# Hybrid decoder block on one core: sparse attention in single key blocks, transposes and products as steps of their own, the first unit beside the last query tile, the compressed product in 128 rows

## The chip, the core and the metric

The kernel runs on one core of a Trainium2 chip. The engines are TensorE (PE, with its weight loads listed as PEld), VectorE (DVE), ScalarE (ACT), GpSimd (POOL) and SyncE (SP), which issues the DMAs. Each engine works through its own queue in the order in which it was written. The metric is the device time of one execution in microseconds, the median over runs.

## The reference

One layer of a decoder block on 1024 tokens with 1024 channels. Two branches read one projection of x: a gated delta rule (o_a, 512 channels) and native sparse attention (o_b, 512 channels). With 16 blocks of 64 keys in the sequence and the 16 best chosen, every block is chosen, so the selected branch is plain causal attention over all keys.

```python
def masked_softmax(s, mask):
    s = jnp.where(mask, s.astype(jnp.float32), -jnp.inf)
    m = jnp.max(s, axis=-1, keepdims=True)
    p = jnp.exp(s - jnp.where(jnp.isfinite(m), m, 0.0))
    d = jnp.sum(p, axis=-1, keepdims=True)
    return p / jnp.where(d > 0, d, 1.0)
...
kc = compress(k_c, pos_k, w1_k, w2_k)          # 63 compressed keys and values
vc = compress(v_c, pos_v, w1_v, w2_v)
p_cmp = masked_softmax(q @ kc, cmp_end <= pos)     # 8 query heads on 2 key heads, 64 channels each
o_cmp = p_cmp @ vc
o_slc = masked_softmax(q @ ks, kpos <= pos) @ vs   # the selected blocks
o_win = masked_softmax(q @ kw, (kpos <= pos) & (kpos > pos - 512)) @ vw
o_b = gt[..., 0:1] * o_cmp + gt[..., 1:2] * o_slc + gt[..., 2:3] * o_win
...
mixed = sigmoid(gate_a) * (o_a @ w_branch_gdn) + sigmoid(gate_b) * (o_b @ w_branch_nsa)
h = layer_norm(DN_ALPHA * x + mixed @ w_out, ln1_g, ln1_b)
u = causal_dwconv(h @ w_up, ffn_conv_w)
u_g, u_v = split(u, 2)
x = layer_norm(DN_ALPHA * h + (silu(u_g) * u_v) @ w_down, ln2_g, ln2_b)
```

## The kernel before

A float32 value is handled as a high and a low part, both in the type that PE takes at full speed; a product is high x high, low x high and high x low. Names that end in h and l, or wh and wl, are such pairs.

The stages follow one another: projections and the delta rule (to about 604 us), the last query tile `q_tile(3)` beside the compression of the values `comp_c("v")` (to 628), the attention (to about 892), the two branch products (to 982), the product with w_out and the norm, the feed-forward (to 1708), and the last norm.

The attention runs over 16 units (t, g): a tile t of 128 queries and a key head g with its four query heads r. The order is `UNITS`: t = 1 to 7, and t = 0 last. A unit has three branches: b = 0, the selected one, over all keys up to its own; b = 1, the window, over at most 640 keys; and the compressed one, over 64 columns.

- `score_steps` makes the scores of one branch. `kS` holds the keys with their high and low halves stacked in 128 rows, `qS` the queries likewise; each head takes two products for its keys (two again where there are more than 512), and a product of the identity with a mask from `am`. DVE takes the maximum (L912), ACT the exponential into P (L914), then DVE the reciprocal of the sum, and `scale` multiplies P by it, on POOL (L876) or ACT (L872) in a rotation, `SCALE`.
- `cmp_scores` does it for the compressed keys (`khc`, `klc`), with two clamps of the statistics (L934, L939), and POOL scales `Pc` (L941).
- `pv_steps` makes an item for each block of 128 keys and one for the compressed ones: four transposes of P on PE into a small PSUM bank (L949), a copy to the high part wh on ACT (L951), a subtraction to the low part wl on DVE (L952), and two products with `vS`, which holds the value's high and low halves side by side. For the compressed item all that has 64 rows and the values are `vC`. The products are held back by `LAG` = 2 items. `weave` lays the items of the unit before among the score steps of a unit. `fin` adds the two halves into `oB`.
- `down_sums` uses POOL (L999) to prepare differences of w_down for the feed-forward, one piece at a time.
- Beside the last unit's items comes the first branch product, `branch(0, 0)`, `Y0` = 4 matmuls ahead of each item. Its inputs are the high and low parts of o_a (`oAh`, `oAl`), split by `half_split` (L1033 to L1036) on ACT, DVE and POOL, and weights that `load_ab` loads, casts on ACT (L1051) and subtracts on POOL (L1052). Then `oB` is split too, and the rest of the branches follow; `use` multiplies by the gates on DVE (L1065).

PSUM has big banks of 1024 columns (`big`) and small ones of 512 (`sm`). Tiles with the tag "wh" or "wl" share a ring of three buffers each; a tile waits until the last use of the one that had its buffer. Inside `manual_schedule` a program orders each engine's queue. The profile names L192, a helper, for every product.

## Time and profile before

| what | value |
|---|---|
| median of 3 runs | 1729.74 us (1729.28 to 1729.77) |
| profiled execution | 1731.17 us |
| its span, first to last instruction | 1729.5 us |
| mean granted clock of TensorE | 0.991 |
| PE busy | 1684.3 us, 97% |
| DVE busy | 1153.4 us, 67% |
| ACT busy | 743.6 us, 43% |
| POOL busy | 783.1 us, 45% |
| DMA moved | 189.90 MB |

The profile is of one execution. The busy time of PE counts the modelled ends of its matmuls: in a run without waits a product of 512 columns shows 0.39 us, and the next one starts 0.23 us after it. So starts, rather than durations, tell what a product costs. The releaser in square brackets is what the profile takes to have ended an engine's idle time. A granted clock of 1.00 is 2.4 GHz, 0.5 is 1.2 GHz.

### The profile page before, as it was taken

What the parts mean: (1) busy time and instruction counts of PE and PEld (TensorE: products, weight loads), DVE (VectorE), ACT (ScalarE), POOL (GpSimd) and SP (SyncE); (2) the same over time, 40 slices, a digit from 0 to 9 for tenths busy, and PEclk for the clock granted to TensorE, in tenths of its full rate; (3) what the DMA queues carried; (4) which work ended last, traced back from release to release, by engine and by line L of the source; (5) the groups of instructions that cost most, each with busy time, mean ns of one, the idle gap of its engine ahead of it and who ended that gap; (6) DMA issues with size and microseconds to landing.
All of it is one profiled execution on the core that took longest, in us unless ns stands there. A gap on an engine that the chain in (4) does not pass through costs nothing.

```text
span 1729.5 us, 23653 instructions
## 1 busy us (share of the span) xinstructions
PE 1684.3 (97%) x8578; PEld 1412.4 (82%) x8578; DVE 1153.4 (67%) x2148; ACT 743.6 (43%) x1280; POOL 783.1 (45%) x650
## 2 busy tenths in 40 slices
PE   8999999999999999999989999999999999999997
PEld 8888888888888877788868787778888888888885
DVE  3556767677644359999863328988777767865756
ACT  3422323323213458788853114544444444543333
POOL 1322222222222537876458226687787777200005
PEclk9999999999999999999999999999999999999998
DMA  5222122121321323333026612333332233597722
GB/s 176 74 63 76 56 61 57 52 75 32 88 80 51 98 88 113 120 118 103 8 85 189 220 49 98 97 122 100 120 116 92 98 103 105 190 362 237 231 94 98
DMA packets 196722, 189.90 MB, mean 110 GB/s; under 512 B 19400, under 2 KB 154749, under 8 KB 196605
## 3 DMA queue, kind: packets, MB, share of 16 engines
q1 hardware_dynamic: 196605, 188.39, 34.3%
q8 instruction: 68, 1.11, 0.3%
q14 instruction: 49, 0.40, 0.1%
HBM read 136.97 MB, written 51.38 MB: 109 GB/s over the span
## 4 chain that ended last, share of the span: by engine, by line
PE 84%; DVE 7%; issue 3%; ACT 3%; POOL 2%; DMA 1%; SPq 0%; ACTq 0%; POOLq 0%; DVEq 0%
PE pq L192 34%; PE big L192 33%; PE sm L192 13%; PE sm L949 3%; DVE st L912 1%; ACT P L914 1%; DVE wl L952 1%; DVE wb L1396 0%; POOL h L1253 0%; POOL hr L1725 0%; POOL h L1254 0%; DMA w<-in_w_out_dram 0%; DVE accs L1407 0%; DMA w<-in_w_in_dram 0%; ACT wh L951 0%
## 5 line engine op out<-in xcount | busy, mean ns | idle before, releaser
L182 POOL TENSOR_TENSOR wl<-w,wh 128x1024 fp32r<-128x1024 f32 (+2 forms) x51 | 123.1, 2420 | 362.0 <-PE big L192 131.0
L192 PE MATMUL big<-xTl,wh 128*128 128x512 f32 x624 | 250.6, 402 | 0.0
L192 PE MATMUL big<-xTh,wh 128*128 128x512 f32 x624 | 250.3, 401 | 0.0
L192 PE MATMUL pq<-wd 128*128 128x512 f32 x924 | 209.6, 389 | 0.0
L192 PEld LDWEIGHTS pq<-wd 128*128 128x128 f32 x924 | 173.5, 188 | 36.0
L192 PE MATMUL pq<-xb,wb 128*128 128x512 f32 x792 | 187.6, 391 | 2.1 <-DVE accs L1407 1.5
L1407 DVE SCALAR_TENSOR_TENSOR accs<-pq,fcw,accs 128x511 f32<-128x511 f32 (+3 forms) x264 | 144.3, 568 | 61.0 <-ACT accs L1495 56.1
L192 PEld LDWEIGHTS pq<-xb,wb 128*128 128x128 f32 x792 | 148.5, 188 | 34.8 <-issue 2.9
L192 PE MATMUL big<-xTh,wl 128*128 128x512 f32 x624 | 164.1, 399 | 0.0
L192 PEld LDWEIGHTS big<-xTl,wh 128*128 128x128 f32 x624 | 117.7, 189 | 21.3 <-issue 0.2
L192 PEld LDWEIGHTS big<-xTh,wh 128*128 128x128 f32 x624 | 117.7, 189 | 21.2
L192 PEld LDWEIGHTS big<-xTh,wl 128*128 128x128 f32 x624 | 114.0, 188 | 22.0
L192 PE MATMUL pq<-mTh,wb 128*128 128x512 f32 x528 | 126.1, 394 | 3.2 <-ACT mTh L1195 3.1
L192 PE MATMUL pq<-mTl,wb 128*128 128x512 f32 x528 | 127.3, 391 | 0.0
L876 POOL TENSOR_TENSOR P<-P,st 128x640 f32<-128x640 f32 (+7 forms) x96 | 99.8, 1068 | 52.6 <-DVE st L885 20.7
L192 PEld LDWEIGHTS pq<-mTh,wb 128*128 128x128 f32 x528 | 100.0, 190 | 25.4 <-ACT mTh L1195 3.3
L192 PEld LDWEIGHTS pq<-mTl,wb 128*128 128x128 f32 x528 | 99.1, 188 | 21.2
L1396 POOL TENSOR_TENSOR wb<-w,wb 128x512 fp32r<-128x512 f32 x79 | 103.5, 1316 | 27.4 <-ACT wb L1195 27.4
L181 ACT ACTIVATE wh<-w 128x1024 fp32r<-128x1024 f32 (+2 forms) x51 | 53.0, 1046 | 128.1 <-PE big L192 85.9
L952 DVE TENSOR_TENSOR wl<-sm,wh 128x512 fp32r<-128x512 f32 (+1 forms) x148 | 99.4, 682 | 10.3 <-ACT wh L951 8.0
L951 ACT ACTIVATE wh<-sm 128x512 fp32r<-128x512 f32 (+1 forms) x148 | 87.1, 595 | 22.7 <-PE sm L949 19.1
L914 ACT ACTIVATE P<-big,st 128x640 f32<-128x640 f32 (+7 forms) x128 | 88.8, 701 | 10.3 <-DVE st L912 9.6
(381 smaller groups left out, 3599.0 us busy)
## 6 DMA issues: line engine op xcount, KB each, us to landing
w<-in_w_in_dram SPq DMA_DIRECT2D x40, 512.0 KB, 4.1
w<-in_w_up_dram SPq DMA_DIRECT2D x36, 512.0 KB, 3.8
w<-in_w_down_dram SPq DMA_DIRECT2D x53, 256.0 KB, 3.2
wsum<-w SPq DMA_DIRECT2D x44, 256.0 KB, 2.5
sig<-th SPq DMA_DIRECT2D x32, 256.0 KB, 2.4
w<-sig SPq DMA_DIRECT2D x16, 512.0 KB, 3.4
wx<-in_w_up_dram SPq DMA_DIRECT2D x11, 512.0 KB, 3.9
gdrC<-accs SPq DMA_DIRECT2D x11, 512.0 KB, 2.6
```

Source lines behind the costliest of these rows:

```text
L181: A.activation(wh[:, :n], w[:, :n], AF.Copy)
L182: G.tensor_tensor(wl[:, :n], w[:, :n], wh[:, :n].bitcast(F32), op=OP.subtract)
L192: PE.matmul(o, a, b, start=start, stop=stop, skip_group_check=True)
L876: G.tensor_tensor(p, p, r.to_broadcast([128, p.shape[1]]), op=OP.mult)
L912: V.reduce_max(nm, pv if m > 1 else pv[:, 0], axis=AX.X, negate=True)
L914: A.activation(P[:, r0 + i, :n], pv[:, i], AF.Exp, bias=nm[:, i:i + 1], accum_out=su[:, i:i + 1])
L949: PE.transpose(tp[:n, r * 128:(r + 1) * 128], P[:, r, c0:c0 + n], ident)
L951: A.activation(ph, tp[:n], AF.Copy)
L952: V.tensor_tensor(pl, tp[:n], ph.bitcast(F32), op=OP.subtract)
L1396: e.tensor_tensor(H.tile[:, 1], src(), H.tile[:, 0].bitcast(F32), op=OP.subtract)
L1407: V.scalar_tensor_tensor(o, i, fcw[:, 2 - s, j:j + 1], o, op0=OP.mult, op1=OP.add)
```

## The change

- `pv_steps`: the transposes with the split (`turn`) and the held products (`flush`) are separate steps of the weave. High and low part of an item are the two halves of one tile, taken by turns from the rings "wh" and "wl", so six buffers serve the items.
- The compressed keys and values lie twice, in rows 0 to 63 and 64 to 127 (`kC`, `vC`). The high part of Pc goes to rows 0 to 63 and the low part to 64 to 127 of one tile, and one product of 128 rows does both.
- Over 512 keys, the scores of a head are made in two equal halves, 640 as twice 320.
- The first unit's scores are made inside `q_tile(3, True)`, which now uses small banks, with `comp_c("v")`.
- The clamps remain for t = 0 alone. `SCALE` gives ACT every sixth operation rather than every fourth; `down_sums` uses three POOL operations for four.
- `half_split` becomes `split_high` and `split_low`. The high parts of o_a are made in unit (0, 0), the low ones at the start of (0, 1), all on POOL; the low parts of o_b all on DVE.
- Beside the last unit's items lie branches (0, 0), (1, 0) and (2, 0), 10 matmuls ahead of each item and 12 after the last. The very last branch writes two small banks.
- Some later tiles change their pools (the weights of w_out, the h tiles, xb3 to xb5), and the last residual rows are loaded after another step.

```diff
-SCALE = "GGGA"
+SCALE = "GGGGGA"
...
+        if t == 1 and g == 0:
+            P = stream.tile([128, 4, 256], F32, name=f"P{b}", tag=("wh", "wl")[b])
...
+            nc_ = n if n <= 512 else n // 2
+            o = 0 if n <= 512 else 512 - nc_
+            pv = ps.rearrange("p (m c) -> p m c", m=m)[:, :, o:o + n]
...
-                for c0 in range(0, n, 512):
-                    c1 = min(n, c0 + 512)
+                for c0 in range(0, n, nc_):
+                    c1 = c0 + nc_
...
-        V.tensor_scalar(nm, nm, 1e29, None, op0=OP.min)
+        if t == 0:
+            V.tensor_scalar(nm, nm, 1e29, None, op0=OP.min)
...
+        def prod(i, vv, parts):
+            if i == 0:
+                s["o"] = sm()
+            for k, p in enumerate(parts):
+                last = i == len(todo) - 1 and k == len(parts) - 1
+                mm(s["o"], vv, p, i == 0 and k == 0, last)
+            if last:
+                fin()
+
+        def turn(i, P, c0, n, vv):
             tp = sm()
             for r in range(4):
                 PE.transpose(tp[:n, r * 128:(r + 1) * 128], P[:, r, c0:c0 + n], ident)
-            ph, pl = htile("wh")[:n, :512], htile("wl")[:n, :512]
+            x = htile(("wh", "wl")[i % 2])
+            if n == 64:
+                parts = [x[:, :512]]
+                ph, pl = x[:64, :512], x[64:, :512]
+            else:
+                parts = ph, pl = x[:, :512], x[:, 512:]
             A.activation(ph, tp[:n], AF.Copy)
             V.tensor_tensor(pl, tp[:n], ph.bitcast(F32), op=OP.subtract)
+            pend.append(functools.partial(prod, i, vv, parts))
...
+            steps += [functools.partial(turn, i, *x), functools.partial(flush, LAG)]
...
+            G.tensor_tensor(b[:, 0:2], b[:, 1:4:2], b[:, 0:2], op=OP.subtract)
+            for o, x, y in ((3, 3, 0), (2, 2, 3)):
...
     with tc.manual_schedule(engines=MS):
-        for t, g in UNITS:
+        s = stats(*UNITS[0])
+        along(q_tile(3, True), itertools.chain(comp_c("v", sv), first_unit(s)))
+        oB = S6.tile([128, 4, T], F32, name="oB", tag="s")
+        pairs, n0 = pv_steps(s)
+        for t, g in UNITS[1:]:
             s = stats(t, g)
             down_sums()
+            if (t, g) == (0, 0):
+                split_high(gA, "A", S6, [A, V])
+            if (t, g) == (0, 1):
+                load_ab(0, wtile)
+                split_low(gA, "A", S6, G)
...
+        def fill():
+            yield from branch(0, 0)
+            load_ab(1, wtile)
+            yield from branch(1, 0)
+            yield from branch(2, 0)
+        y0 = fill()
+        for i, p in enumerate(pairs):
+            for _ in range(0 if i % 2 else Y0):
                 next(y0, None)
+            p()
+        load_ab(2, wtile)
+        for _ in range(Y1):
+            next(y0, None)
+        flush()
+        split_high(oB, "B", S2b, [A, V])
+        split_low(oB, "B", S2b, V)
         for _ in y0:
             pass
```

What follows are rows of the engines' queues; a name is followed by a number where several tiles share it. First PE at the end of `q_tile(3)`, whose products read xTh and xTl. kS_4955 and qS_4664 (4954 and 4663 after) are the first unit's keys of branch 0 and its queries. Before:

```order
L192 MATMUL big<-xTh_83,wl 128x512 x8
L192 MATMUL big<-xTh_85,wl 128x512 x8
L192 MATMUL big<-kS_4955,qS_4664 128x256 x2
...
L192 MATMUL sm<-am,identr 128x256
L192 MATMUL sm<-khc,qS_4664 128x64
L192 MATMUL sm<-klc,qS_4664 128x64
...
L192 MATMUL big<-kS_5160,qS_4664 128x256 x2
```

After:

```order
L193 MATMUL sm<-xTl_86,wh 128x512
L193 MATMUL big<-kS_4954,qS_4663 128x256 x2
...
L193 MATMUL sm<-xTh_83,wl 128x512 x2
L193 MATMUL sm<-am,identr 128x256
L193 MATMUL sm<-kC,qS_4663 128x64 x8
L193 MATMUL sm<-xTh_83,wl 128x512
L193 MATMUL big<-kS_5159,qS_4663 128x256 x2
...
L193 MATMUL sm<-xTh_83,wl 128x512 x5
L193 MATMUL sm<-xTh_85,wl 128x512 x8
```

The first unit's scores moved into the query tile's products, which moved from a big bank to small ones.

Second, PE among the scores of one early unit, where P_5484 (before) and P_5476 (after) hold the branch 0 of the unit before it. Before:

```order
L949 MATMUL sm<-ident,P_5484 128x128 x4
L192 MATMUL sm<-wh,vS 128x512
L192 MATMUL sm<-wl,vS 128x512
L192 MATMUL big<-kS_5160,qS_4664 128x384 x2
...
L949 MATMUL sm<-ident,P_5484 128x128 x4
L192 MATMUL sm<-wh,vC 128x512
L192 MATMUL sm<-wl,vC 128x512
L192 MATMUL big<-kS_4955,qS_5019 128x384 x2
```

After:

```order
L985 MATMUL sm<-ident,P_5476 128x128 x4
L193 MATMUL sm<-wl,vS 128x512 x2
L193 MATMUL big<-kS_5159,qS_4663 128x384 x2
...
L985 MATMUL sm<-ident,P_5476 128x128 x4
L193 MATMUL sm<-wh,vC 128x512
L193 MATMUL big<-kS_4954,qS_5018 128x384 x2
```

The order of items and scores is the same; high and low part come from one tile, and the second compressed product is gone.

Third, POOL at the last two units. P0_8243, Pc_8383 and P1_8391 (before), Pw_8069 and Pc_8200 (after) belong to unit (0, 0); P0_8472, Pc_8534 and P1_8542 (before), Pw_8301 and Pc_8361 (after) to (0, 1). Before:

```order
L876 TENSOR_TENSOR P0_8243<-P0_8243,st_8242 128x128 x3
L941 TENSOR_TENSOR Pc_8383<-Pc_8383,st_8242 128x256
L876 TENSOR_TENSOR P1_8391<-P1_8391,st_8242 128x128 x3
L876 TENSOR_TENSOR P0_8472<-P0_8472,st_8471 128x128 x3
L1036 TENSOR_TENSOR oAl_8580<-gA_590,oAh_8579 128x512 x4
L1052 TENSOR_TENSOR wl_8598<-w_8599,wh_8597 128x512
L941 TENSOR_TENSOR Pc_8534<-Pc_8534,st_8471 128x256
```

After:

```order
L874 TENSOR_TENSOR Pw_8069<-Pw_8069,st_8059 128x128 x3
L1062 TENSOR_TENSOR oAl_8292<-gA_590,oAh_8060 128x512 x8
L950 TENSOR_TENSOR Pc_8200<-Pc_8200,st_8059 128x256
L874 TENSOR_TENSOR Pw_8069<-Pw_8069,st_8059 128x128 x3
L1078 TENSOR_TENSOR wl_8283<-w_8284,wh_8282 128x512 x2
L874 TENSOR_TENSOR Pw_8301<-Pw_8301,st_8281 128x128 x4
L950 TENSOR_TENSOR Pc_8361<-Pc_8361,st_8281 128x256
```

The low parts of o_a moved one unit ahead, from the last unit's compressed scaling to the one before's, and are eight on POOL instead of four.

## Rows read from the trace of the kernel before

**Rows 1.** The page's first part: busy time of each engine in us, its share of the span, and instructions.

```profile
PE 1684.3 (97%) x8578; PEld 1412.4 (82%) x8578; DVE 1153.4 (67%) x2148; ACT 743.6 (43%) x1280; POOL 783.1 (45%) x650
```

**Rows 2.** Busy time by stretch: from and to, length, busy us and instructions of PE, PEld, DVE, ACT and POOL, granted clock, share of the DMA engines, GB/s.

```profile
650.00:850.00 200.00, 196.12 (x1248) 166.28 (x1249) 184.52 (x337) 168.10 (x350) 145.71 (x156) 1.00 0.30 98
850.00:900.00 50.00, 42.35 (x244) 33.53 (x243) 38.06 (x70) 33.47 (x87) 26.94 (x30) 0.94 0.19 59
950.00:1000.00 50.00, 48.43 (x211) 39.20 (x210) 18.12 (x19) 9.99 (x14) 15.93 (x9) 1.00 0.65 225
1050.00:1708.00 658.00, 651.81 (x2879) 536.72 (x2878) 487.66 (x738) 293.90 (x437) 350.32 (x273) 1.00 0.43 143
1708.00:1729.50 21.50, 9.59 (x43) 7.61 (x41) 11.53 (x24) 5.07 (x7) 10.69 (x11) 0.79 0.33 122
```

**Rows 3.** The same columns for three stretches at the lower clock.

```profile
635.00:638.40 3.40, 3.40 (x19) 3.40 (x19) 2.07 (x6) 1.75 (x8) 2.15 (x4) 0.50 0.00 0
880.80:884.20 3.40, 3.40 (x9) 2.53 (x10) 3.40 (x3) 2.69 (x11) 3.40 (x3) 0.50 0.37 141
897.80:901.20 3.40, 3.40 (x9) 2.62 (x8) 0.55 (x1) 0.63 (x1) 3.40 (x4) 0.50 0.38 123
```

**Rows 4.** PE's timeline in a middle unit: start, length, line, operation, output and inputs, partitions x columns, count.

```profile
781.96 0.63 PE L949 MATMUL sm<-ident,P 128*128 128x128 f32 x4
782.34 0.48 PE L192 MATMUL sm<-wh,vS 128*128 128x512 f32 x1
782.66 0.39 PE L192 MATMUL sm<-wl,vS 128*128 128x512 f32 x1
782.89 0.80 PE L192 MATMUL big<-kS,qS 128*128 128x512 f32 x4
783.53 0.39 PE L192 MATMUL big<-am,identr 128*128 128x128 f32 x2
783.76 0.62 PE L949 MATMUL sm<-ident,P 128*128 128x128 f32 x4
784.31 0.50 PE L192 MATMUL sm<-wh,vC 64*128 64x512 f32 x1
784.65 0.39 PE L192 MATMUL sm<-wl,vC 64*128 64x512 f32 x1
784.97 0.91 PE L192 MATMUL big<-kS,qS 128*128 128x512 f32 x4
```

**Rows 5.** Groups of instructions between 560 and 1010 us, by shape: busy us in all, mean ns of one, then the idle time before them.

```profile
L952 DVE TENSOR_TENSOR wl<-sm,wh 128x512 fp32r<-128x512 f32 x132 | 88.7, 683 | 7.8 <-ACT wh L951 5.7
L999 POOL TENSOR_TENSOR w<-w 128x256 f32<-128x256 f32 x88 | 64.3, 736 | 24.0 <-DMA w<-in_w_down_dram 15.0 <-issue 3.7 <-POOL P L876 1.2
L876 POOL TENSOR_TENSOR P<-P,st 128x640 f32<-128x640 f32 x30 | 36.8, 1255 | 15.1 <-DVE st L885 8.0 <-ACT wh L951 5.0 <-PE big L192 2.1
L912 DVE TENSOR_REDUCE st<-big 128x1 f32<-128x640 f32 x40 | 32.5, 812 | 1.1 <-PE big L192 0.9
L939 DVE TENSOR_SCALAR st<-st 128x4 f32<-128x4 f32 x16 | 6.7, 418 | 0.1
L934 DVE TENSOR_SCALAR st<-st 128x4 f32<-128x4 f32 x16 | 5.5, 342 | 0.1
L1036 DVE TENSOR_TENSOR oAl<-gA,oAh 128x512 fp32r<-128x512 f32 x4 | 5.4, 1385 | 0.0
L1036 DVE TENSOR_TENSOR oBl<-oB,oBh 128x512 fp32r<-128x512 f32 x4 | 3.7, 961 | 0.0
```

**Rows 6.** Timelines of PE, then of DVE, around the first unit's window scores. In square brackets: idle time before, and what ended it.

```profile
630.56 0.28 PE L192 MATMUL sm<-klc,qS 128*128 128x64 f32 x1
633.82 0.47 PE L192 MATMUL big<-kS,qS 128*128 128x256 f32 x2 [2.98 <-DVE qS L728]
...
632.44 1.23 DVE L728 SCALAR_TENSOR_TENSOR qS<-big,qS 64x1024 fp32r<-64x1024 f32 x1
```

**Rows 7.** PE's timeline: the longest wait between 640 and 855 us.

```profile
672.98 0.60 PE L949 MATMUL sm<-ident,Pc 128*64 128x128 f32 x4 [1.09 <-DVE wl L952]
```

**Rows 8.** Timelines of PE, of ACT and of POOL in the last unit and behind it.

```profile
880.80 2.08 PE L192 MATMUL big<-oAh,wh 128*128 128x512 f32 x4 [2.29 <-ACT wh L1051]
886.86 0.63 PE L949 MATMUL sm<-ident,Pc 128*64 128x128 f32 x4 [1.10 <-POOL Pc L941]
891.89 2.02 PE L192 MATMUL big<-oAl,wh 128*128 128x512 f32 x8
896.35 0.50 PE L192 MATMUL big<-oAh,wh 128*128 128x512 f32 x1 [2.44 <-ACT wh L1051]
...
878.57 1.66 ACT L1035 ACTIVATE oBh<-oB 128x512 fp32r<-128x512 f32 x3
880.13 0.62 ACT L1051 ACTIVATE wh<-w 128x512 fp32r<-128x512 f32 x1
893.50 2.19 ACT L1035 ACTIVATE oBh<-oB 128x512 fp32r<-128x512 f32 x4 [0.76 <-DVE oB L971]
...
877.59 6.32 POOL L1036 TENSOR_TENSOR oAl<-gA,oAh 128x512 fp32r<-128x512 f32 x4
```

**Rows 9.** PE's timeline at the end of the branch products.

```profile
978.66 0.50 PE L192 MATMUL big<-oBh,wh 128*128 128x512 f32 x1 [0.78 <-DVE w L1065]
982.48 0.50 PE L192 MATMUL pq<-woh,mTh 128*128 128x512 f32 x1 [0.79 <-DVE w L1065]
```

More of the change, by code (lines that the diff above doesn't have):

```diff
@@ L1009, in down_sums, with first_unit, split_high @@
             held.append((b, k, cs))
-    prev = None
     pend = []
     LAG = 2
-    with tc.manual_schedule(engines=MS):
-        for t, g in UNITS:
+    def first_unit(s):
+        for b in range(2):
+            for f in score_steps(s, b):
+                f()
+                for _ in range(4):
+                    yield
+            if b == 0:
+                cmp_scores(s)
+                yield
+    oT, wab, sg = {}, {}, {}
+    def split_high(src, nm_, pool, engines):
+        hi = oT[nm_, "hi"] = pool.tile([128, 4, T], F32R, name=f"o{nm_}h", tag="s")
+        for hf, hs in enumerate(HS):
+            oT[nm_, "h", hf] = hi[:, :, hs]
+            for k in range(4):
+                if engines[k % len(engines)] is V:
+                    V.tensor_copy(hi[:, k, hs], src[:, k, hs])
+                else:
+                    A.activation(hi[:, k, hs], src[:, k, hs], AF.Copy)
@@ new lines, in split_low, with load_ab @@
+    def split_low(src, nm_, pool, engine):
+        hi = oT[nm_, "hi"]
+        lo = pool.tile([128, 4, T], F32R, name=f"o{nm_}l", tag="s")
+        for hf, hs in enumerate(HS):
+            oT[nm_, "l", hf] = lo[:, :, hs]
+            for k in range(4):
+                engine.tensor_tensor(lo[:, k, hs], src[:, k, hs], hi[:, k, hs].bitcast(F32), op=OP.subtract)
+    def load_ab(j, get):
+        jc = slice(j * 128, j * 128 + 128)
+        wh, wl = htile("wh"), htile("wl")
+        full = get() if get is wtile else None
+        for i in range(2):
+            w = full[:, HS[i]] if full is not None else get()
+            wv = w.rearrange("p (k c) -> p k c", c=128)
+            if i == 0:
+                nc.sync.dma_start(wv, w_a.rearrange("(k p) c -> p k c", p=128)[:, :, jc])
+            else:
+                for g in range(2):
+                    nc.sync.dma_start(wv[g * 64:g * 64 + 64],
+                                      w_b[g * 256:(g + 1) * 256, jc].rearrange("(r d) c -> d r c", d=64))
+            A.activation(wh[:, HS[i]], w, AF.Copy)
+            G.tensor_tensor(wl[:, HS[i]], w, wh[:, HS[i]].bitcast(F32), op=OP.subtract)
+        wab[j] = wh, wl
@@ L1055, in branch @@
+            pairs, n0 = pv_steps(s)
         def branch(j, i):
[L1056 removed]
+            last = (i, j) == (1, KT - 1)
+            ps = (sm(), sm()) if last else big()
             ws = ktiles(*wab[j], i * 4, i * 4 + 4)
             xs = {(p, hf): oT["AB"[i], p, hf] for p in "hl" for hf in range(2)}
[L1059 to L1065 removed]
+            if (j, i) == (0, 1):
+                parts = [cg.tile([128, 512], F32, name="wab", tag="wab") for _ in HS]
+            else:
+                t = wtile()
+                parts = [t[:, hs] for hs in HS]
+                sg[i, j] = t
@@ new lines, in branch @@
+            for p, hs in zip(parts, HS):
+                nc.sync.dma_start(p, sig[i * 8 + j][:, hs])
+            def use(hs):
+                if (j, i) == (0, 1):
+                    for p, h in zip(parts, HS):
+                        V.tensor_tensor(p, ps[:, h], p, op=OP.mult)
+                        V.tensor_tensor(sg[0, j][:, h], sg[0, j][:, h], p, op=OP.add)
+                else:
+                    V.tensor_tensor(t[:, hs], ps[HS.index(hs)] if last else ps[:, hs], t[:, hs], op=OP.mult)
@@ L1344, in h4 @@
             if 4 not in XB:
[L1345 removed]
+                XB[4] = S6.tile([128, 2, 4, 512], F32R, name="xb4", tag="s")
             hi(4, tt, t4)(_)
@@ L1587, in hybrid_block_kernel @@
     final = groups[-1]
-    for n in (1, 6, 7, 5, 2, 3):
+    for n in (1, 6, 7, 2, 4):
         P.add("X", 0, lambda _: None, [final.n[n]], lat=0, grow=[("slot", [0])])
+    P.add("X", 0, lambda _: None, [final.n["end"], groups[-2].n["free"]], lat=0, grow=[("slot", [0])])
     for i in range(10):
@@ L1608, in f @@
             nc.sync.dma_start(hrest(t), hres[t])
-        return P.add("S", 1.8, f, [final.n[4]] if t < 4 else [final.n["end"], groups[-2].n["free"]], lat=2.0)
+        return P.add("S", 1.8, f, [final.n[3]], lat=2.0)
     def load_l2(src, hs):
```

166 lines of the change are left out of this document (58 added, 108 removed).

## The prediction

> **What bounds the kernel now.** I read the busy times first: TensorE (PE) is busy 97% of the span, VectorE (DVE) 67%, GpSimd (POOL) 45% [rows 1]. So time is won by taking work off PE or by closing PE's waits, and by nothing else. Next I cut the span into stretches [rows 2]. From 1050 to 1708 us PE has 6 us idle in 658; that is the merge, the norm and the feed-forward, in which the change reorders almost nothing on PE. What is gained earlier is therefore passed on to the end, and what other engines gain is worth nothing unless PE waits for them. In the attention units (650 to 850) PE idles 3.9 us in 200 while DVE is busy 184.5, ScalarE (ACT) 168 and POOL 146. From 850 to 900, the last units, PE idles 7.65 us in 50, and from 950 to 1000 another 1.6. The granted clock says the rest: three stretches of 3.4 us stand at 0.5, which is the 1.2 GHz level, all next to PE's longest waits [rows 3]; each costs 1.7 us of full-speed work. The last 21.5 us (DVE and POOL rows of the final norm, PE 9.6 busy) I leave as they are. The loads of its residual rows are released earlier, but the chain that ended last runs there through DVE and POOL, not through a load, so I give them nothing, with 2 us either way in the range.
>
> The sum goes against the profiled execution: span 1729.5, execution 1731.17, which is 1.43 above the median of the runs, 1729.74. I take the sum from 1731.17 and then 1.43 off. A time within 0.2% (3.5 us) of 1729.74 counts as no change.
>
> **1. Compressed product in 128 rows.** An ordinary item is four transposes, a high and a low product. In the timeline it starts at 781.96, the products at 782.34 and 782.66, the next work at 782.89: steps of 0.38, 0.32 and 0.23, 0.93 together. The compressed item is 783.76, 784.31, 784.65, 784.97: 0.55, 0.34 and 0.32, 1.21 together [rows 4]. So changing between 128 and 64 rows costs PE about 0.17 on the way in and 0.09 on the way out, beside a product that moves only half the rows in the same time. After the change one product of 128 rows follows the transposes: 0.38, and then 0.23 to 0.32 to the next work. I take 0.32, since this product is a first one after transposes: 0.70. Saved 0.51, for 16 units (L934 runs once in each) [rows 5]: **8.2 us**. Bounds: if only one product's streaming goes and the two row changes stay, 16 x 0.23 = 3.7; if 0.23 holds, 9.6. The work on ACT and DVE stays one copy and one subtraction.
>
> The Trainium skill, "TensorEngine Tiling (Array Packing)", Tiling Modes, says that changing the tiling mode drains TensorE. Taken alone, that rule would put a drain also at the compressed transposes, which have 64 weight columns, and the 0.17 would then stay (5.5 us saved); the trace has the delay at the 64-row products.
>
> **2. Scores in equal halves.** For 640 keys a head is two products of 512 columns and two of 128: from 782.89 to the mask product at 783.53, 0.64 [rows 4]. Four of 320 at 0.23/512 a column are 4 x 0.144 = 0.58. Saved 0.06 in each of 40 heads (L912) [rows 5]: **2.4 us**. For 768 and 896 keys the columns only divide otherwise, 512 + 256 is as long as twice 384: nothing. Bounds 0 (if the short products already hid behind the long ones' weight loads) and 4.
>
> **3. First unit beside the last query tile.** Before, PE ends the compressed scores at 630.56 + 0.11 and starts the window scores at 633.82, since their PSUM bank is held until DVE's second evacuation of query tile 3, from 632.44 for 1.23 us [rows 6]: 3.15 us lost. The half clock at 635.0 follows and costs 1.7 [rows 3]: 4.85 in reach. After the change tile 3 lies in small banks and its products stand between the first unit's score groups (the first order rows in the section on the change), so the bank is no longer waited for. Late next: the second unit's scores need the last head of the tile, one half evacuation on ACT and one on DVE (about 0.6 each, half of the 1.23) after the last product of the tile, with an exponential or two of the first unit ahead on ACT: I estimate 1.8 us of waiting. Whether the clock then falls again I count with 1.05, a little over half of 1.7. 4.85 - 1.8 - 1.05 = **2 us**, bounds 0 and 4.85.
>
> **4. Transposes and products as steps of their own, six buffers for three; less on DVE.** The two clamps go from 14 of 16 units: 14 x (0.342 + 0.418) = 10.6 us off DVE [rows 5], which is the fullest engine beside PE in 650 to 850. ACT hands about 11 scalings to POOL (about 1.26 each at 640 keys [rows 5]: some 14 us), and the weight sums give some back: 22 times one operation of twice the size for two of 0.736, a saving of 0 to 16 us. POOL has 54 us free there, so I cost this at nothing; were it not so, the transposes of Pc and P would wait for POOL. PE has 3.9 us of idle time to give back, and each wait costs some 0.17 beyond its idle time, because a product shows 0.40 busy while the next may start after 0.23. Some dozen waits, the longest 1.09 at 672.98 [rows 7]: about 6 in reach. I take half: **3 us**, bounds 0 and 6.
>
> **5. The last units.** Four causes stand in the timelines [rows 8]. At 880.80 PE has waited 2.29 for ACT's cast of the first branch weights: three casts of oBh (878.57, 1.66) were queued ahead of the cast at 880.13. At 886.86 it has waited 1.10 for Pc, which on POOL stands behind four subtractions for oAl (877.59, 6.32 together). At 896.35 it has waited 2.44 for the next weights, whose cast stands behind four casts of oBh (893.50, 2.19). Two half clocks come with them [rows 3]. In reach: 7.65 idle in 850 to 900 and 1.6 in 950 to 1000 (two waits of 0.8 for a bank that DVE still reads [rows 9], which the two small banks end), 3.4 for two half clocks, and 12 x 0.17 = 2: 14.6 us.
> The change casts oA one unit earlier and loads the weights ahead. 72 products on oA now stand among and behind the last unit's items, where 24 did: 48 more, at 0.23 some 11 us of PE work that waits for nothing of the last unit, while its output is added, cast and subtracted. That work is moved, not added. What stays: POOL now does all eight oAl ahead of the compressed scaling and the window scaling of unit (0,0) (the last order rows), 8 x 1.58 = 12.6 us from 877.59's row. PE meanwhile has the items of unit (7,1), some 11 x 0.9 us, and scores: I count 1.5 us of wait. Behind the last item oB needs an addition and casts on both engines (about 4 us) and eight subtractions on DVE at 0.961 [rows 5], 7.7 us, of which the first is needed after 16 products more than the oA ones: about 1. ACT's casts of oA ahead of an evacuation: 0.7. 14.6 - 3.2 = **11.4 us**, bounds 4 (two of the four waits stay, with their half clocks) and 14.6.
> The Trainium skill, "SBUF — State Buffer", SBUF: two separate sides, speaks against this: a GpSimd operation and a VectorE operation with two SBUF inputs exclude each other on a shared port pair. The trace agrees: the DVE part of oAl took 1.385 beside POOL's, oBl 0.961. By that rule oBl, which runs beside POOL's weight splits, takes 8 x 1.385 = 11.1, 3.4 more than in my sum.
>
> **Sum.** 8.2 + 2.4 + 2 + 3 + 11.4 = 27.0. 1731.17 - 27.0 = 1704.2 for the profiled execution, 1702.7 for the median.
>
> **Rivals.**
> (a) The forecast, 1702.7, from 1698 to 1707: 0.58.
> (b) The end keeps its waits: eight oAl on POOL hold Pc and P of unit (0,0) longer than the items of (7,1) last, PE stands, and the clock falls to 0.5 once or twice as it does now. End gain 4: 19.6 in all, 1710.1. For it: POOL's order is fixed and 12.6 us is longer than PE's 10 us of items. Against: scores and the compressed items lie between. 0.15.
> (c) Little but PE's work comes home: parts 3 and 4 give 0, because the waits move to ACT and POOL (more scalings there, DVE no longer the last), and the end gives 4: 14.6, 1715.1. For it: 6 us in reach of part 4 is a sum of small waits. 0.10.
> (d) The row change isn't what costs: part 1 gives 3.7, in all 22.5, 1707.2. 0.06.
> (e) DVE and POOL hold each other up on oBl, +3.4: 23.6, 1706.1. 0.04.
> (f) More than the sum, all at its upper bounds (9.6 + 4 + 4.85 + 6 + 14.6 = 39): below 1698. 0.03.
> (g) Slower: with products in steps of their own each item's product follows its evacuation too closely, and PE waits at every item. There are 132 items of keys (L952) [rows 5] and 16 compressed ones; from 27.0/148 = 0.18 us an item the whole gain is gone, at 0.25 the time is 1739.7. Against: the lag of two items is kept, the buffers double, and in 781 to 785 items run without a wait while DVE is fuller than it will be. 0.04.
>
> **Numbers.** Forecast 1702.7; its own range 1698 to 1707. The range that leaves out under 2 in 10 reaches from 1696, between (a) and the upper bounds, to 1716, past (c). Faster by over 0.2%: all but (g) and a scrap for mishaps between, 0.93; within 0.2%: 0.03; slower: 0.04.
>
> **What would show it.** Part 1: the step from the transposes to vC near 0.38 and no second product. Part 2: 0.58 for a head of 640. Part 3: no wait over 2 us between 625 and 640, no bank held by DVE's qS. Part 4: PE idle under 2.5 us over the 200 us of the middle units. Part 5: no 0.5 in the clock after 850, PE idle under 4 us from 850 to the merge. The prediction is wrong if the transposes of Pc or P wait for POOL in the last two units for several us, if PE waits for wh or wl at many items, or if the tail after PE's last product grows.

## The result and the profile after

The changed kernel takes 1721.62 us (median of 6 runs, 1717.89 to 1725.35), the kernel before beside it 1731.32: ratio 0.9939, 95% interval 0.9925 to 0.9952. By the ratio that is 10.6 us (8.3 to 13.0), by the medians 9.7, where 27.0 were forecast; 1721.62 lies outside the range. Ratios below are against runs of the kernel before that were taken beside each version. In the profiled executions the last product on PE starts at 1717.20 before and 1706.88 after, 10.3 us earlier.

The page of the changed kernel, first part, answers to [rows 1]:

```profile
PE 1673.9 (97%) x8562; PEld 1410.5 (82%) x8562; DVE 1154.6 (67%) x2129; ACT 734.3 (43%) x1269; POOL 787.5 (46%) x640
```

PE's busy time fell by 10.4 us. DVE's, from which two clamps in 14 units had gone, didn't fall. By stretch, as in [rows 2] and [rows 3]:

```profile
650.00:850.00 200.00, 191.36 (x1262) 167.22 (x1260) 186.16 (x319) 166.05 (x352) 152.62 (x148) 1.00 0.33 105
850.00:900.00 50.00, 45.87 (x237) 38.25 (x238) 32.95 (x60) 25.99 (x69) 28.95 (x34) 0.90 0.23 69
950.00:1000.00 50.00, 50.00 (x221) 41.21 (x220) 16.51 (x20) 10.14 (x14) 14.01 (x8) 1.00 0.65 221
851.70:855.10 3.40, 2.85 (x11) 2.55 (x12) 2.38 (x4) 1.72 (x4) 3.37 (x5) 0.50 0.00 0
868.80:875.60 6.80, 6.80 (x31) 6.14 (x30) 2.42 (x5) 3.06 (x12) 4.26 (x8) 0.50 0.00 0
```

In the middle units PE idles 8.6 us of 200 where it idled 3.9: PE got less work and waits longer. The waits between 950 and 1000 are gone. Between 620 and 1000 us the clock stands at 0.5 for 10.2 us, as long as before (3 times 3.4), only elsewhere.

**Landmarks.** Where the work goes is read from marks in PE's timeline. The mask product at the head of each unit's compressed scores is such a mark; after:

```profile
638.30 0.28 PE L193 MATMUL sm<-am,identr 128*128 128x256 f32 x1
836.64 0.28 PE L193 MATMUL sm<-am,identr 128*128 128x256 f32 x1
859.07 0.28 PE L193 MATMUL sm<-am,identr 128*128 128x256 f32 x1
874.35 0.41 PE L193 MATMUL sm<-am,identr 128*128 128x256 f32 x1
972.24 0.40 PE L193 MATMUL pq<-woh,mTh 128*128 128x512 f32 x1
```

These are units (1,1), (7,1), (0,0) and (0,1), and the first product with w_out. The same four units before, where the first product with w_out stands at 982.48 [rows 9]:

```profile
640.60 0.28 PE L192 MATMUL sm<-am,identr 128*128 128x256 f32 x1
842.95 0.28 PE L192 MATMUL sm<-am,identr 128*128 128x256 f32 x1
863.13 0.28 PE L192 MATMUL sm<-am,identr 128*128 128x256 f32 x1
875.12 0.28 PE L192 MATMUL sm<-am,identr 128*128 128x256 f32 x1
```

Ahead of them, the same products with w2s stand at 619.26 before and 618.25 after, and the first transposes of P at 637.96 and 634.94. The stretches between:

| stretch | before | after | gained | forecast there |
|---|---|---|---|---|
| start to 619 | | | 1.0 | 0 |
| 619 to the first transposes of P | | | 2.0 | 2 (part 3) |
| to (1,1) | 2.6 | 3.4 | -0.7 | 0 |
| middle: (1,1) to (7,1) | 202.35 | 198.34 | 4.0 | 6.1 + 2.2 + 3 (parts 1, 2, 4) |
| (7,1) to (0,1) | 32.17 | 37.71 | -5.5 | 1.2 (parts 1, 2), and part 5 |
| (0,1) to w_out | 107.36 | 97.89 | 9.5 | 1 (part 1); part 5 in both rows, 11.4 |

So of some 11.3 us due in the middle 4 came, and the stretch from (7,1) to (0,1) took back more than half of what came behind it. The first row is no gain of the change: it arises in the first 17 us, whose work is the same, and where the kernel before stood at the lower clock for 6.8 us in its profile. Of the -5.5, 4.5 are the lower clock of the rows above; of the 9.5, 2.8 are lower clock that is no longer there. Below, a stretch is also given with half of its time at the lower clock taken off, as "at full clock", since that part falls differently in each execution.

**Parts 1 and 2 themselves** are as forecast. After, in one unit:

```profile
781.12 0.74 PE L193 MATMUL big<-kS,qS 128*128 128x320 f32 x4
781.70 0.33 PE L193 MATMUL big<-am,identr 128*128 128x128 f32 x2
...
778.04 0.47 PE L193 MATMUL sm<-wh,vC 128*128 128x512 f32 x1
779.32 0.85 PE L193 MATMUL big<-kS,qS 128*128 128x320 f32 x4 [0.81 <-ACT P L921]
```

A head of 640 keys takes 0.58 to its mask, not 0.64. One compressed product is left, but in this unit PE waits 0.81 us behind it for ACT's exponentials, which free the score bank: more than the 0.51 by which the item got shorter.

**Part 3** went as told in one respect: PE waits 1.00 for the second unit's scores and 0.90 for the first products with P, both for DVE's evacuation of the tile's last head, and the clock stayed at 1.00. A third wait, 1.15, stands ahead of them: PE waits for `vC`, which ACT and DVE now write twice, and before there was no wait at this product:

```profile
622.81 0.45 PE L193 MATMUL sm<-w2s,hTc 128*64 128x64 f32 x4 [1.15 <-DVE vC L826]
634.54 0.50 PE L193 MATMUL big<-kS,qS 128*128 128x256 f32 x2 [1.00 <-DVE qS L728]
637.33 0.47 PE L193 MATMUL sm<-wh,vS 128*128 128x512 f32 x1 [0.90 <-DVE qS L728]
```

**The two last units.** PE, POOL and DVE in unit (0,0):

```profile
867.37 0.51 PE L193 MATMUL sm<-wh,vS 128*128 128x512 f32 x1 [1.75 <-DVE wh L993]
...
858.02 9.91 POOL L1062 TENSOR_TENSOR oAl<-gA,oAh 128x512 fp32r<-128x512 f32 x8 [2.94 <-PE sm L985]
867.88 0.62 POOL L950 TENSOR_TENSOR Pc<-Pc,st 128x256 f32<-128x256 f32 x1
...
860.66 1.14 DVE L942 TENSOR_SCALAR st<-st 128x4 f32<-128x4 f32 x1
864.51 0.98 DVE L883 TENSOR_TENSOR st<-st,gates 128x4 f32<-128x4 f32 x1
865.61 1.10 DVE L883 TENSOR_TENSOR st<-st,gates 128x4 f32<-128x4 f32 x1
866.63 0.68 DVE L993 TENSOR_TENSOR wh<-sm,wh 128x512 fp32r<-128x512 f32 x1
```

The block of oAl took 9.9 us, where 12.6 were reckoned, but PE did not wait for POOL's scaling behind it. Three of DVE's operations on 4 columns took about 1 us each while it ran, where the same take 0.16 elsewhere; the evacuation that PE waits for is queued behind them, and the clock falls at 868.8. Experiment 6 takes the block away from there.

### The profile page after: what moved, and what is told of

Same layout as the page of the kernel before. It is cut to its first block, busy times and chain, and to the rows that moved or that the text cites. A ratio compares the mean times of both kernels' runs of the same rounds, so it can differ in the third digit from the quotient of the medians.

```text
span 1719.1 us, 23524 instructions
## 1 busy us (share of the span) xinstructions
PE 1673.9 (97%) x8562; PEld 1410.5 (82%) x8562; DVE 1154.6 (67%) x2129; ACT 734.3 (43%) x1269; POOL 787.5 (46%) x640
## 4 chain that ended last, share of the span: by engine, by line
PE 79%; DVE 9%; issue 4%; DMA 3%; POOL 3%; ACT 3%; SPq 0%; ACTq 0%; POOLq 0%; DVEq 0%
PE pq L193 35%; PE big L193 29%; PE sm L193 12%; PE sm L985 2%; DVE st L919 1%; DVE wh L993 1%; POOL P L874 1%; ACT P L921 1%; DMA wsum<-w 1%; DVE st L883 1%; DMA w<-in_w_out_dram 1%; DVE wl L993 1%; DVE wb L1455 0%; DVE accs L1466 0%; DMA w<-in_w_down_dram 0%
## 5 line engine op out<-in xcount | busy, mean ns | idle before, releaser
L193 PE MATMUL big<-xTl,wh 128*128 128x512 f32 x608 | 244.0, 402 | 0.0
L193 PE MATMUL big<-xTh,wh 128*128 128x512 f32 x608 | 244.0, 401 | 0.0
L1466 DVE SCALAR_TENSOR_TENSOR accs<-pq,fcw,accs 128x510 f32<-128x510 f32 (+3 forms) x264 | 144.4, 568 | 61.0 <-ACT accs L1554 56.1
L193 PE MATMUL big<-xTh,wl 128*128 128x512 f32 x608 | 160.3, 399 | 0.0
L874 POOL TENSOR_TENSOR P<-P,st 128x640 f32<-128x640 f32 (+6 forms) x94 | 106.4, 1161 | 43.6 <-DVE st L883 20.2
L193 PE MATMUL big<-kS,qS 128*128 128x320 f32 (+5 forms) x384 | 86.4, 342 | 3.4 <-ACT P L921 2.2
L1254 ACT ACTIVATE wb<-w 128x512 fp32r<-128x512 f32 x85 | 53.3, 629 | 80.9 <-PE pq L193 76.1
L921 ACT ACTIVATE P<-big,st 128x640 f32<-128x640 f32 (+6 forms) x112 | 83.3, 749 | 10.3 <-DVE st L919 10.0
```

Of the source, the lines that this page charges most:

```text
L193: PE.matmul(o, a, b, start=start, stop=stop, skip_group_check=True)
L874: G.tensor_tensor(p, p, r.to_broadcast([128, p.shape[1]]), op=OP.mult)
L921: A.activation(P[:, r0 + i, :n], pv[:, i], AF.Exp, bias=nm[:, i:i + 1], accum_out=su[:, i:i + 1])
L1254: A.activation(o, i, AF.Copy)
L1466: V.scalar_tensor_tensor(o, i, fcw[:, 2 - s, j:j + 1], o, op0=OP.mult, op1=OP.add)
```

## The experiments

**1. The compressed product alone.** Into the kernel before, whose values `vC` are then also written twice (cut):

```diff
...
+            if n == 64:
+                x = htile("wh")
+                ph, pl, parts = x[:64, :512], x[64:, :512], [x[:, :512]]
...
+                for k, p in enumerate(parts):
+                    mm(s["o"], vv, p, first and k == 0, last and k == len(parts) - 1)
```

> The kernel before, with the compressed item alone changed: its low part goes to rows 64 to 127 of one tile and one product of 128 rows replaces two of 64. Theory PE work: the step from the transposes to the product falls from 0.55 to about 0.36 us, the second product goes, 0.51 us in each of 16 units, and all of it arrives: 8 us faster than before (1731 to 1723). Rival, PE waits for others: the attention units run at the pace of the chain DVE, ACT and POOL, the item gets shorter by 0.51 but PE's waits in the middle units grow by half of it or more: 2 to 5 us faster.

Measured: 1726.48 beside 1730.61, ratio 0.9971 (0.9960 to 0.9982): 5.0 us by the ratio, 4.1 by the medians. In the middle, 202.35 became 200.58: 1.8 of the 6.1 us due in 12 units. The timeline shows where the rest went:

```profile
782.80 0.62 PE L951 MATMUL sm<-ident,P 128*128 128x128 f32 x4
783.18 0.47 PE L192 MATMUL sm<-wh,vC 128*128 128x512 f32 x1
784.30 0.90 PE L192 MATMUL big<-kS,qS 128*128 128x512 f32 x4 [0.64 <-ACT P L916]
```

The step to vC is 0.38 as reckoned, not 0.55, and the second product is gone: PE's work did shrink by 0.51. But 0.64 of waiting follows. The rival of the expectation came. From 650 to 850 us PE idles 6.8 us, where it idled 3.9 [rows 2]:

```profile
650.00:850.00 200.00, 193.25 (x1252) 166.44 (x1252) 186.33 (x341) 170.32 (x355) 146.54 (x158) 1.00 0.30 98
```

Another loss lies ahead of the attention. From the first product with w2s to (1,1) this kernel takes 22.74 us, before 21.34. The only edit there is that ACT and DVE write `vC` twice beside the query tile; the wait for the tile's evacuation, 2.98 in [rows 6], became longer:

```profile
636.43 0.48 PE L192 MATMUL big<-kS,qS 128*128 128x256 f32 x2 [3.94 <-DVE qS L728]
```

**2. DVE relieved.** In the kernel before, and with experiment 1, the maximum over fewer keys:

```diff
-            V.reduce_max(nm, pv if m > 1 else pv[:, 0], axis=AX.X, negate=True)
+            V.reduce_max(nm, pv[:, :, n - 128:n] if m > 1 else pv[:, 0, n - 128:n], axis=AX.X, negate=True)
```

> The kernel before, with each head's maximum taken over its last 128 keys alone (the maximum only shifts the exponent; the part of it over the other keys is left out). DVE loses some 50 of its 184 us in the middle units, and nothing else changes. Theory PE alone: PE is busy 196 of 200 us there, so 2 to 5 us faster than before. Rival, both at the limit: the same, since PE has only its 4 us to give; this run is the base for the next one.

> The same short maximum, with the compressed product in 128 rows. Theory, DVE took the gain: with DVE far from its limit the 8 us of PE work arrive whole, 7 to 9 us faster than the run with the short maximum alone, against 4 without it. Rival, the score banks or ACT took it: ACT is as full as before (168 of 200), PE still waits for P after the compressed item, and only 4 to 5 us arrive.

Measured: 1736.27 (ratio 1.0031, 1.0016 to 1.0045) and 1722.58 (0.9954, 0.9937 to 0.9971). The short maximum alone is slower than before by 5 us; 2.2 of that lie ahead of unit (1,1), where PE waits once for ACT's copy. I hadn't expected a loss, and can't account for all of it. The two from 650 to 850, with the columns of [rows 2]:

```profile
650.00:850.00 200.00, 196.11 (x1251) 166.10 (x1250) 143.51 (x334) 165.14 (x352) 145.07 (x157) 1.00 0.31 98
650.00:850.00 200.00, 194.99 (x1268) 168.29 (x1267) 148.81 (x344) 168.74 (x358) 146.81 (x159) 1.00 0.31 98
```

In the middle, at full clock, they take 202.2 and 198.5. With DVE full (184 to 186 of 200 us) the 128 rows bring 1.8 of 6.1 us there, with DVE at 144 to 149 they bring 3.7. So DVE's load on the chain from scores to a free bank kept some 2 of the 4.3 us that were missing; what kept the other 2.4 isn't shown. Each of these figures is from one profile, and two profiles of one kernel differ by 1.0 in this stretch (experiment 4). From (1,1) to the first product with w_out it is 3.8 against 7.9, but there 2.1 and 3.6 come behind (0,1), where the item is worth 1.0, so other waits moved too. The medians differ by 13.7 us, more than the 8.2 that the product can save: the base had lost time of its own, and this difference is no measure of the product.

**3. Clamps alone**, in the kernel before: both under `if t == 0`, as in the change.

> The kernel before, with the two clamps kept for t = 0 alone. Theory work: the 14 x (0.34 + 0.42) = 10.6 us are DVE's own work; DVE's busy time in the units falls by 10.6, the gate multiplication of the statistics (128x4, two SBUF inputs) stays at 0.25 us, and the time falls by 1 to 3 us. Rival, waiting: the small operations take about 0.17 us by themselves and the rest is waiting while POOL works on SBUF; without the clamps the gate multiplication behind them takes over the wait, 48 of them rise from 11.6 us to 16 to 20 in all, and the time stays within 1 us.

Measured: 1729.32, ratio 0.9993 (0.9984 to 1.0002), no difference that can be told. The gate multiplications rise from 11.6 to 13.7 us, so only a fifth of the 10.6 us passes to them. The rival had the time right and its reason wrong: most of the clamps' time did leave DVE in the middle, and was worth 1.4 us there.

**4. Less waiting of DVE for POOL**, in the changed kernel. The gate multiplication on POOL, a scaling in four on ACT, four small weight sums:

```diff
-        V.tensor_tensor(s["rr"][:, b], s["rr"][:, b], s["gt"][:, b], op=OP.mult)
+        G.tensor_tensor(s["rr"][:, b], s["rr"][:, b], s["gt"][:, b], op=OP.mult)
...
-    SCALE = "GGGGGA"
+    SCALE = "GGGA"
...
-            G.tensor_tensor(b[:, 0:2], b[:, 1:4:2], b[:, 0:2], op=OP.subtract)
-            for o, x, y in ((3, 3, 0), (2, 2, 3)):
+            for o, x, y in ((0, 1, 0), (1, 3, 1), (3, 3, 0), (2, 2, 3)):
```

> The changed kernel, with the 48 gate multiplications of the statistics (128x4) on POOL instead of DVE. Theory waiting: in the changed kernel they take 22.6 us on DVE, of which some 15 are waiting for POOL operations; on POOL they run in its own order. DVE is free 20 us more, PE's waits for DVE's evacuations between 635 and 870 us shrink, 3 to 6 us faster than the changed kernel (1713 to 1717 where that has 1720). Rival, POOL's queue: POOL's order is what delays, the multiplications stand behind its sums and scalings and every P comes later; 2 to 6 us slower than the changed kernel.

> The changed kernel with every fourth scaling on ACT again, as before, instead of every sixth. If the 13 us more on POOL cost the middle units their gain (its operations hold up DVE's small ones): the gate multiplications fall from 0.47 us toward 0.30 and the time by 2 to 4 us. Rival, ACT is fuller than POOL there: 1 to 3 us slower. If the share doesn't matter: within 1 us.

> The changed kernel with four small operations of 0.74 us for the weight sums instead of one of 1.29 and two small ones. If POOL's longer operations hold up DVE's small ones: the gate multiplications fall from 0.47 us to 0.40 or less and the time by 0.5 to 2 us. If POOL's busy time counts: 4 us more of it, 0 to 1 us slower.

> The changed kernel with the gate multiplications on POOL and four small operations for the weight sums. Both take waits off DVE or shorten them: together 2 to 5 us faster than the changed kernel (1714 to 1718). If the second only helped by DVE's waits, which are gone with the first: as the gate multiplications alone, 1719.

> The changed kernel with both of its POOL edits undone: every fourth scaling on ACT, four small operations for the weight sums. Theory: these two are what the middle units paid for; alone they brought 198.3 us from (1,1) to (7,1) down to 196.9 (with 1.7 of lower clock in it) and 196.4, together 193 to 195, and the time is 3 to 6 us shorter than the changed kernel's. Rival: the middle is held by DVE's order whatever POOL does, 196 to 198, time within 2 us of the changed kernel's.

> The changed kernel with every fourth scaling on ACT and the gate multiplications on POOL. Theory, both only shorten DVE's waits for POOL: as one of them alone, 195 to 197 us from (1,1) to (7,1), 1716 to 1720. Rival, independent: 192 to 194 there, 1713 to 1717.

| changed kernel with | median | ratio (interval) | middle | at full clock | gate multiplications |
|---|---|---|---|---|---|
| nothing, first profile | 1721.62 | 0.9939 (0.9925 to 0.9952) | 198.3 | 198.3 | 0.470 us, DVE |
| nothing, again | 1722.84 | 0.9954 (0.9942 to 0.9967) | 202.4 | 197.3 | 0.440, DVE |
| multiplication on POOL | 1719.02 | 0.9922 (0.9907 to 0.9938) | 196.8 | 195.1 | 0.205, POOL |
| a scaling in four on ACT | 1721.18 | 0.9949 (0.9931 to 0.9968) | 196.9 | 195.2 | 0.417, DVE |
| four small sums | 1718.05 | 0.9928 (0.9916 to 0.9940) | 196.4 | 196.4 | 0.433, DVE |
| multiplication, sums | 1724.22 | 0.9961 (0.9948 to 0.9973) | 199.5 | 196.1 | 0.204, POOL |
| scaling, sums | 1722.63 | 0.9963 (0.9949 to 0.9978) | 200.0 | 196.6 | 0.365, DVE |
| scaling, multiplication | 1721.03 | 0.9944 (0.9932 to 0.9956) | 199.2 | 195.8 | 0.206, POOL |

Each takes 1 to 3 us from the middle at full clock, where the two profiles of the changed kernel itself differ by 1.0. They don't add up: with scaling and sums together, as the rival said, the middle stays at 196.6. The whole time follows none of it beyond the intervals, and a lower clock falls elsewhere in several of these profiles. The multiplication's two rows, changed kernel and then on POOL:

```profile
L883 DVE TENSOR_TENSOR st<-st,gates 128x4 f32<-128x4 f32 x48 | 22.6, 470 | 0.9
```

```profile
L883 POOL TENSOR_TENSOR st<-st,gates 128x4 f32<-128x4 f32 x48 | 9.7, 205 | 47.7 <-DVE st L882 45.6 <-ACT P L921 2.1
```

On DVE it is mostly waiting. No version of these is shown to beat the changed kernel.

**5. Separate steps.** Transposes and products as one step again:

```diff
-            steps += [functools.partial(turn, i, *x), functools.partial(flush, LAG)]
-        return steps, 2 * (t + 2)
+            steps.append(lambda i=i, x=x: (turn(i, *x), flush(LAG)))
+        return steps, t + 2
...
-            for _ in range(0 if i % 2 else Y0):
+            for _ in range(Y0):
```

> The changed kernel with an item's transposes and the held products as one step of the weave again (the six buffers stay). If separate steps help, as I had counted (3 us with the buffers): 1 to 3 us slower than the changed kernel. If it is them that let PE wait at the items: 1 to 3 us faster. The order of PE hardly moves, so I expect within 1 us.

Measured: 1719.99, ratio 0.9944 (0.9929 to 0.9959), the same. In the middle it needs 200.7 at full clock, 2 to 3 us more than with separate steps, and it happened to have no time at the lower clock behind (7,1). In this profile, then, the steps help there, as I had counted; the whole time doesn't tell.

**6. The block of oAl.** By turns on DVE and POOL:

```diff
-                split_low(gA, "A", S6, G)
+                split_low(gA, "A", S6, [V, G])
```

Later, behind unit (0,0)'s scaling:

```diff
-                split_low(gA, "A", S6, G)
...
             cmp_scores(s)
+            if (t, g) == (0, 1):
+                split_low(gA, "A", S6, G)
```

Left out, with the high parts read in place of the low ones:

```diff
-                split_low(gA, "A", S6, G)
+                oT["A", "l", 0], oT["A", "l", 1] = oT["A", "h", 0], oT["A", "h", 1]
```

> The changed kernel with the eight low parts of o_a by turns on DVE and POOL, as before the change, instead of all on POOL. Theory, POOL's block of 10 us costs the last units: it becomes 5 to 6 us long, DVE's small operations are held up less, PE's longest wait in unit (0,0) (1.75 us) falls under 1, and the clock keeps 1.0 from 865 on: 2 to 4 us faster than the changed kernel. Rival, DVE's four (1.0 to 1.4 us each) come ahead of the evacuations instead: no gain, or 1 to 2 us slower.

> The changed kernel with the low parts of o_a made later: their tile is taken after the one of unit (0,1)'s P, so it gets its buffer when unit (7,1)'s items are through, and on POOL they stand behind the compressed and window scaling of unit (0,0). Theory, the block ahead of that scaling and beside DVE's small operations is what unit (0,0) pays for: its compressed scores to the next unit's fall from 15.3 to about 12 us, no 0.5 in the clock there, 3 to 4 us faster than the changed kernel. Rival, the block only moves: the scaling of unit (0,1) or the first products on the low parts wait for it, and 1 us or less is left.

> The changed kernel without the eight low parts of o_a (the products read the high parts in their place, so a small part of the result is wrong and the PE work is the same). Theory, POOL's block costs the end its gain: (0,0) to (0,1) takes 11 to 12 us instead of 15.3, the clock stays at 1.0 there, 4 to 5 us faster than the changed kernel. Rival, the last units wait as much for DVE's evacuations without it: 1 us or less.

> The changed kernel with the gate multiplications on POOL and the low parts of o_a by turns on DVE and POOL. If both act on different places: the gain of the multiplications (2.6 us) and that of the low parts add up, 1713 to 1717. If POOL's block was the place of both: as the multiplications alone, 1719.

> The low parts of o_a later, and the gate multiplications on POOL. If the two act on different places (the middle units, and unit (0,0)): 2.6 and 3.5 us, 1713 to 1716, faster than the changed kernel and than before. If POOL's queue takes back what DVE gives: as the better one alone.

Measured, in this order: 0.9968 (0.9956 to 0.9980), 0.9967 (0.9955 to 0.9979), 0.9968 (0.9958 to 0.9978), 0.9931 (0.9915 to 0.9946), 0.9935 (0.9922 to 0.9948); medians 1725.39, 1725.38, 1724.59, 1718.82 and 1719.73. None is shown to help, and the last two are as the multiplication alone (0.9922). With DVE taking part PE waits in unit (0,0) for DVE:

```profile
868.64 1.09 PE L985 MATMUL sm<-ident,P 128*128 128x128 f32 x4 [4.06 <-DVE wl L993]
```

With the block later, (0,0) to (0,1) takes 10.7 us instead of 15.3, as expected. The operations on 4 columns that had taken 1.14, 0.98 and 1.10 us in this unit are short again:

```profile
860.51 0.17 DVE L942 TENSOR_SCALAR st<-st 128x4 f32<-128x4 f32 x1
863.58 0.16 DVE L883 TENSOR_TENSOR st<-st,gates 128x4 f32<-128x4 f32 x1
864.18 0.34 DVE L883 TENSOR_TENSOR st<-st,gates 128x4 f32<-128x4 f32 x1
```

But the next unit pays:

```profile
879.92 1.55 PE L985 MATMUL sm<-ident,Pw 128*128 128x128 f32 x4 [3.96 <-POOL Pw L874]
```

Without it, the same operations take 0.17, 0.17 and 0.34, and (0,0) to (0,1) also falls to 10.6, but the loads shift with the buffers, DVE waits 12.3 us for a gate from memory, and PE 5.8 for DVE:

```profile
916.31 1.23 DVE L1120 TENSOR_TENSOR w<-big,w 128x1024 f32<-128x1024 f32 x1 [12.32 <-DMA w<-sig]
```

So the price of the block in unit (0,0) is shown, 4.6 us against the first profile of the changed kernel with its lower clock, 2.0 against the second, which has none there (12.7); and it is shown that DVE's small operations wait beside it. None of these places for it is free.

**7. The changed kernel again, and with DVE relieved** (the short maximum of experiment 2):

> The changed kernel itself, once more, as the base of the runs beside it: 1718 to 1722, with a wait of some 2 us in unit (0,0) and the clock at 0.5 behind it.

> The changed kernel with each head's maximum over its last 128 keys alone (the rest of the maximum is left out), which takes some 40 of 187 us off DVE in the middle units. Theory, DVE near its limit keeps the PE work that the change saves: from the compressed scores of (1,1) to those of (7,1) it takes 192 to 195 us where the changed kernel takes 198.3 and before 202.4, and the time is 3 to 6 us shorter than the changed kernel's. Rival, the waits come from ACT, POOL or the order itself: within 1.5 us of 198.3.

Measured on one chip beside each other: 1722.84, ratio 0.9954 (0.9942 to 0.9967), and 1718.28, 0.9921 (0.9907 to 0.9935): about 5 us from the 43 that DVE was spared in 200. The profiled executions don't show these 5 us: they took 1719.61 and 1719.40. In the middle 197.3 and 196.2 at full clock, so only 1 to 2 of the missing 6 to 7 lie in the maxima there: nearer to the rival than to the theory. PE now waits for DVE's additions of the output (4.2 us) and its evacuations. In the changed kernel the rest of the middle's loss is spread over the evacuations, the output's addition and the score banks, and no single cause was found for it.

The wait in unit (0,0) came back as expected, with the same 1.75 us, but the clock behind it stayed at 1.00:

```profile
869.08 0.50 PE L193 MATMUL sm<-wh,vS 128*128 128x512 f32 x1 [1.75 <-DVE wh L993]
869.00:876.00 7.00, 6.92 (x55) 6.50 (x56) 4.87 (x12) 4.62 (x14) 5.96 (x11) 1.00 0.00 0
```

## Why the prediction was wrong

Of the 16.7 us between 27.0 and the 10.3 of the first profile, 7.3 are missing in the middle, 9.7 from (7,1) to w_out and 0.7 ahead of (1,1); the start gave 1.0 by chance. Two of the prediction's own signs of failure came: PE idles 8.6 us in the middle units, not under 2.5, and the clock stands at 0.5 after 850.

**Parts 1 and 2 were right as PE's work**: 0.51 us an item and 0.06 a head, 8.2 and 2.4 us. The step that failed is the one from PE's work to time. The prediction says that "what other engines gain is worth nothing unless PE waits for them"; its sum also took for granted that all that PE saves arrives, and had no term for PE starting to wait. Part 1 alone brought 1.8 of its 6.1 us in the middle, and with DVE relieved 3.7 (experiments 1 and 2). So DVE, at 184.5 of 200 us [rows 2], is part of the reason; the rest is open, and no run has part 2 alone. "The work on ACT and DVE stays one copy and one subtraction" holds for an item, but not for the values, which are now written twice: PE waits 1.15 us for them beside the query tile.

**Part 3 came near its 2 us, in part by luck.** The bank is no longer waited for, and the two waits at the end, 1.00 and 0.90, are close to the 1.8 of the estimate. The clock, costed at 1.05, didn't fall in the first profile, but the 1.15 for the values, which the sum didn't have, took that back; up to (1,1), behind the second of the two waits, 1.3 us were gained. In the second profile the clock did fall there, at 638.3 for 3.4 us.

**Part 4 brought about nothing of its 3 us.** In the middle 202.4 less 8.3 for parts 1 and 2 would be 194.1, and at full clock it took 197.3 and 198.3. But that loss can't be put to part 4: with part 1 alone 4.3 us were missing already, and the middle took 200.6. If part 2's 2.2 arrived, 198.4 was left for part 4 to shorten, so it gave 0 to 1. "I cost this at nothing" is not borne out for POOL's added work: undoing either POOL edit takes 1 to 3 us from the middle in single profiles. What I weighed was POOL's free time. DVE's gate multiplications rose from 0.247 to 0.470 us, 11 us in all, as much as the clamps gave back; with both POOL edits undone they still take 0.365, so those edits are only a part of the rise. Separate steps were worth 2 to 3 us in one profile; the waits that the six buffers should have closed were replaced by others, the longest of them 2.29 at 685.13:

```profile
685.13 0.60 PE L985 MATMUL sm<-ident,Pc 128*64 128x128 f32 x4 [2.29 <-DVE oB L970]
...
683.67 0.59 ACT L969 ACTIVATE w<-sm 64x512 f32<-64x512 f32 x1 [2.25 <-POOL w L1021]
```

The output's addition on DVE stands behind this copy on ACT, which waits for a buffer of the weight sums on POOL. It is the one wait of the middle that the runs of experiment 4 trace to POOL's work: with four small sums, or with the multiplication on POOL, it is gone, and with a scaling in four on ACT it is 1.01.

**Part 5: the outcome of rival (b) came, by another path.** Rival (b), given 0.15, said that "PE stands, and the clock falls to 0.5 once or twice", because POOL holds Pc and P. PE did stand, but for an evacuation of DVE, whose small operations waited beside POOL's block. From (7,1) to w_out 3.9 us were gained in the first profile and 8.3 in the second, which kept its clock there, where 11.4 and 2.3 of parts 1 and 2 were forecast, 13.7 together. At full clock it is 5.6 and 4.9 of 10.3. The other 3.4 of the forecast were two half clocks: the second profile got them back, the first lost 1.7 more than before. The stall of 1.5 us was right in size (1.75) by luck, since it was reckoned from POOL's queue; the lower clock behind it the sum had put to 0. The products beside the last unit did what they should: (0,1) to w_out fell by 9.5 us (6.7 at full clock), the waits for the last banks are gone, and those for ACT's casts are down to one of 0.5.

The rival that the prediction took from the Trainium skill on SBUF held in another place than the one I priced. The eight oBl on DVE took 0.819 us each, less than the 0.961 of before, so the 3.4 us didn't come: only one operation of POOL, 1.58 us, ran beside them. The 0.961 was a mixture, too: two of the four took 1.29 us together while POOL was idle, the other two 2.39 beside POOL's half of oBl. But operations of DVE on SBUF beside POOL's did wait, the ones of four columns, and these stand ahead of evacuations. The Trainium skill, "SBUF — State Buffer", section SBUF: two separate sides, says that the loser is blocked for the whole of the other's instruction; the trace agrees, with 0.98 to 1.14 us for operations of 0.16 beside POOL's 1.24, and 0.16 to 0.34 for the same ones once the block is elsewhere (experiment 6).

**Rival (c)**, "little but PE's work comes home", was the nearest: 14.6 us. It failed still, since it let all of PE's work come home.

## What to carry to other kernels

Before work on the busiest engine is priced at full value, look at the next engine's busy time in the same stretch: here, with PE at 98% and DVE at 92%, 1.8 of 6.1 us arrived, and 3.7 with DVE at 72 to 74%. Work moved to POOL is not free when POOL has time; ask what DVE does on SBUF meanwhile, and what is queued behind it. And a stall of 2 us on PE cost its length here and, in some executions, 3.4 us more in the clock, so a term that removes low clock must ask where the next stall is. A run that is to isolate one edit needs a base that didn't lose time of its own, as the one with the short maximum did.

## What was not expected of the hardware

DVE's operations on 128x4 values, 0.15 to 0.18 us by themselves, took about 1 us while POOL worked through 128x512 subtractions, also one with a single input (L942, 1.14; 0.17 with the block elsewhere).

The granted clock falls in one execution and not in another behind the same wait. The wait of 1.75 us in unit (0,0) is one case: 6.8 us at 0.5 behind it in the first profile of the changed kernel, none in the second. The wait of 2.29 us at 685 is another, the other way round: it stands in both, in the first the clock stays at 1.00, in the second:

```profile
685.54 0.60 PE L985 MATMUL sm<-ident,Pc 128*64 128x128 f32 x4 [2.29 <-DVE oB L970]
686.10:692.90 6.80, 6.80 (x27) 5.95 (x26) 4.44 (x10) 3.21 (x8) 6.08 (x7) 0.50 0.53 157
```

That is 3.4 us lost by chance, and the changed kernel's runs spread over 7.5 us.
